# The delta rule's stages ranked 150 places later, background pieces re-spread, 32x32 bursts cut in halves

## The chip, the cores and the metric

The kernel runs on one core of one Trainium2 chip, as one program. The metric is the device time of an execution in microseconds; smaller is better. Times of several runs are given as a median, and traces are of one profiled execution.

## The reference

Two layers of a trunk over 256 tokens of width 2048, with 256 context tokens that only the first layer reads. Both layers take their shifts, scales and gates from a small vector times a large matrix (`w_ada`).

- Layer 0: a windowed attention with 8 heads beside a gated delta rule with 8 heads in two directions, an output projection, then a gated feed-forward block of width 5632.
- Layer 1: a Fourier mix over tokens and channel groups, a projection (`w_fourier`), then a second such feed-forward block.

```python
mx = jnp.split(silu_c @ w_ada[layer] + b_ada[layer], N_MOD, axis=-1)
h_x = modulate(rms_norm(x, g_pre_mix[layer]), mx[0], mx[1])
# layer 0: attention and delta rule, merged by w_out;  layer 1: fourier_mix(h_x) @ w_fourier
x = x + mx[2] * rms_norm(y_x, g_post_mix[layer])
f_x = swiglu(modulate(rms_norm(x, g_pre_ffn[layer]), mx[3], mx[4]), w_gate, w_up, w_down)
x = x + mx[5] * rms_norm(f_x, g_post_ffn[layer])
```

The delta rule works in chunks: each chunk needs a unit triangular solve, `sol = triangular_solve(I + m, rhs)`, and then a short scan over the chunks carries a state from one to the next.

## The kernel before

**Weights.** All large products are made in a split form: each weight tile (`raw`, 128x1024, 512 KB) is loaded on SyncE's queue (L188), copied to a rounded part `whi` on ScalarE (L198) and its remainder `wlo` (L204) on VectorE or GpSimd, and every product is three matmuls (L431 to L435, or L930 to L932). In the mixer of layer 0 `MSHARE` is 1, so GpSimd makes every `wlo` there. A load takes a buffer of the ring `raw` (4 buffers); while no pace is set, two in five take one of `araw` (2 buffers, L187).

**Background pieces.** What the layers need of `silu_c @ w_ada` beyond the first two vectors is cut into 320 pieces (L278 to L292): a load of 512 KB into `araw` on SyncE's queue (L286) and one product with a sum on VectorE (L275). Thirty-two pieces make one modulation vector. They are written into the program at a pace: `every(us)` (L148) says that a piece is written each time the kernel's own clock has gone on by so many microseconds. This clock (L131) is advanced by each matmul as it is written, by its columns over 2400, four times that for plain f32. The mixer's pace is `MRATE` (4.3, after a quiet start of 16), that of the output projection's first three strips `ORATE` (4.0), of layer 0's feed-forward block `F0RATE` (3.9), of the Fourier projection's first three strips `FRATE` (0, none), of layer 1's block `F1RATE` (10). `ada_until(n)` (L303) writes at once whatever is missing of the first n vectors: before the last strip of the output projection n is 3, of layer 0's down projection 6, of the Fourier projection 9 (L1183), and before that projection's first strip 7 (L1407).

**Delta rule.** Heads go in four groups g of two. Stage a (`gdn_a`, L636) makes a group's decay factors, its two sets of triangles and the inverse of their 16x16 blocks on VectorE (L737 to L744), with two trips through DRAM (L722 and L731, L750); stage b (`gdn_b`, L753) grows the inverses from 16 to 32, 64 and 128, and runs the scan over four chunks (L856 to L910). The step from 16 to 32 is made of 32x32 products in plain f32: 64 into `pQ` (L772 to L775), a copy of them to `Q5` (L777), then twice 64 into `pP` (L779 to L788). A stage issues its DMAs on ScalarE's queue, one of four stores of L750 on SyncE's, and its two fills with zeros on GpSimd (L726, L794).

**Order.** Stages, evacuations and attention are generators in a list `todo`; after each step of a projection `step()` (L592) resumes those whose time by the kernel's own clock has come, and what they write is placed there in the program. The number of microseconds that a generator yields, times `YS` = 1.2, is the wait until it is resumed. A planner then orders each engine's instructions: of those that are ready in its own model of the run, it takes the one with the lowest rank, and ranks are given in the order of writing. On VectorE the order is the written one between `in_order(True)` and `in_order(False)`, which holds from the first tile of a feed-forward block to the last strip of its down projection (L1262, L1184); the mixer and the Fourier stage are left to the planner.

Of the kernel before, what the change touches and what calls it, by code (L numbers as in the profile page):

```python
# [38 lines left out]
YF = 18  # L39
ORATE = 4.0  # L40
F0RATE = 3.9
FRATE = 0
F1RATE = 10.0
LD1 = 3
LD2 = 4
LD3 = 3
LD4 = 6
YSUB = 3
MAN = False
MAN2 = True  # L50
YEV = 1.3
# [3 lines left out]
PSPLIT = 0.25  # L55
NACT = 2
MSHARE = 1.0
MRATE = 4.3

WHO = 'pd' * 16  # L60
PRE = (4, 4, 4, 4)
# [11 lines left out]
def trunk(ctx: ExitStack, tc: tile.TileContext, a: dict, dbg=None, stop=None):  # L73
# [10 lines left out]
    def T(shape, tag, bufs, dt=F32):  # L84
        uid[0] += 1
        return sb.tile(list(shape), dt, tag=tag, bufs=bufs, name=f"{tag}_{uid[0]}")
# [28 lines left out]
    def e2(shape, dt=F32):  # L115
        return T(shape, "E2", 3, dt)
# [8 lines left out]
    def sm():  # L125
        uid[0] += 1
        return ps.tile([P, 512], F32, tag="sm", bufs=4, name=f"sm_{uid[0]}")
# [3 lines left out]
    def mm(out, l, r, start, stop):  # L131
        clock[0] += max(64, int(np.prod(r.shape[1:]))) * (4 if r.dtype == F32 else 1) / 2400.0
        nc.tensor.matmul(out, l, r, start=start, stop=stop)  # L133
# [14 lines left out]
    def every(us):  # L148

        pace[:] = [us, clock[0] + us]  # L150
# [3 lines left out]
    def in_order(on):  # L154

        if held:
            held.pop().__exit__(None, None, None)
        if on:
            held.append(tc.manual_schedule(engines={mybir.EngineType.DVE}))
            held[0].__enter__()  # L160
# [136 lines left out]
    def bg(n):  # L297
        for _ in range(n):
            if ada_n[0] < 320:
                next(ada_it)  # L300
                ada_n[0] += 1
# [287 lines left out]
    def add(gen, name=None):  # L589
        todo.append([gen, clock[0], name])  # L590

    def step():  # L592

        while pace[0] and pace[1] <= clock[0]:
            pace[1] += pace[0]
            bg(1)
        for t in list(todo):
            if t[1] <= clock[0]:
                d = next(t[0], None)
                if d is None:  # L600
                    todo.remove(t)
                    done.add(t[2])
                else:
                    t[1] = clock[0] + d * YS

    def drain(name=None):
        if name is not None and name in done:
            return
        while todo and (name is None or name not in done):
            clock[0] = max(clock[0], min(t[1] for t in todo))  # L610
            step()

    def gdn_proj(g):
        for fin, base, n in ((fin_k, 8, 2), (fin_v, 16, 2), (fin_q, 0, 1)):
            for hh in range(2):
                if (base + hh, g) == (8, 1):
                    continue
                p = acc()
                for hf in range(2):
                    w = load_w(a["w_gdn"][base + 2 * g + hh, hf])  # L620
                    for kk in range(8):
                        k = hf * 8 + kk
                        sl = slice(kk % 4 * P, (kk % 4 + 1) * P)
                        if n == 2:
                            mm3w(p, w[kk // 4], sl, k, k == 0, k == KC - 1)
                        else:
                            mm3(p, w[kk // 4], sl, 0, k, k == 0, k == KC - 1, 0)
                        step()
                add(fin(g, hh, p))
        add(gdn_a(g), f"a{g}")  # L630
        add(gdn_b(g), f"b{g}")

    def bl(i, n=32):
        return slice(n * i, n * i + n)

    def gdn_a(g):  # L636
# [100 lines left out]
        for k in range(15, 0, -1):  # L737
# [5 lines left out]
            if k % 4 == 0:  # L743
                yield YSUB  # L744
        V.tensor_copy(Y2[:, 1], Y.rearrange("p r c -> p c r"))
# [7 lines left out]
    def gdn_b(g):  # L753
# [18 lines left out]
        for d in range(2):  # L772
            for e in range(8):
                for b in range(4):
                    mm(pQv[bl(b), d, e], Zc[bl(b), d, e], YD[bl(b), 1, d, e], True, True)  # L775
        Q5 = e2([P, 2, 8, 32])
        V.tensor_copy(Q5, pQv)  # L777
        yield 2
        for i in (1, 0):  # L779
            pP = sm()  # L780
            pPv = pP.rearrange("p (d e f) -> p d e f", d=2, e=8)
            for d in range(2):
                for e in range(8):
                    for b in range(4):
                        x_, y_ = Q5[bl(b), d, e], YD[bl(b), 0, d, e]
                        if i == 1:
                            x_, y_ = y_, x_
                        mm(pPv[bl(b), d, e], x_, y_, True, True)  # L788
            (pP0, pP1) = (pPv, pP1) if i == 0 else (None, pPv)
        for i, p_ in ((0, pP0), (1, pP1)):  # L790
            V.tensor_tensor(out=YD[:, i], in0=YD[:, i], in1=p_, op=ALU.subtract)
# [121 lines left out]
    def proj(warr, npair, lhs, tiles, kept=None, nkeep=0, last=0):  # L913


        out = {t: acc() for t in tiles}
        second = kept is not None and tiles[0] > 0
        ks = range(npair)
        if second and last:
            ks = [npair - 1, *range(npair - 1)]  # L920
        for kp in ks:
            w = kept[kp] if second and kp in kept else load_w(warr[kp])
            if kept is not None and not second and (kp < nkeep or last and kp == npair - 1):
                kept[kp] = w
            for kk, (wh, wl) in enumerate(w):
                k = 2 * kp + kk
                first, final = kp == ks[0] and kk == 0, kp == ks[-1] and kk == 1
                for t in tiles:
                    h, l = lhs(k, t)
                    mm(out[t], h, wh, first, False)  # L930
                    mm(out[t], h, wl, False, False)
                    mm(out[t], l, wh, False, final)  # L932
                    step()
        return out
# [111 lines left out]
    add(fin_k(1, 0, p1))  # L1046
    add(gdn_a(0), "a0")
    add(gdn_b(0), "b0")
    every(MRATE)
    pace[1] += QUIET  # L1050
# [6 lines left out]
    seq.extend(a["w_att"][i, j] for i in range(1, 5) for j in range(8))  # L1057
    in_order(MAN)
    for g in range(1, 4):
# [296 lines left out]
    ab = {}  # L1356

    def over_d(g, t):

        if t == 0:  # L1360
            if g % 3 == 0:
                ab[0] = [zt([P, 3, 258], F32R) for _ in range(2)]
            dst = [ab[0][i][:, g % 3] for i in range(2)]
        else:
            r_ = T([P, 2, 258], "OG", 2, F32R)
            dst = [r_[:, i] for i in range(2)]
        ab[g, t] = dst
        p = sm()
        i = 0
        for kc in range(2):  # L1370
            src = hsl(2 * g + kc, t)
            for x_, y_ in three:
                mm(p[:, 0:258], src[x_], DD[y_][:, kc, :], i == 0, i == 5)
                i += 1
        split(*dst, p[:, 0:258])
# [19 lines left out]
    for g in range(9):  # L1395
# [6 lines left out]
        for h in range(FAHEAD, 8):  # L1402
            if g == h - 2:
                over_d(h, 0)
    every(FRATE)
    pool_share[0] = 0.0
# [123 lines left out]
```

## Time and profile before

| | us |
|---|---|
| median of 3 runs | 2509.49 |
| lowest and highest run | 2507.83, 2510.64 |
| the profiled execution | 2512.88 |
| its span in the trace | 2511.1 |
| TensorE matmul busy | 2386.3 (95%) |
| VectorE busy | 1778.5 (71%) |
| ScalarE busy | 1286.7 (51%) |
| GpSimd busy | 303.5 (12%) |

The profiled execution is 3.4 us (0.13%) above the median. In the trace the mixer lies from about 165 to 765 us, the output projection from 768 to 860, layer 0's feed-forward block up to about 1600, the Fourier transforms from 1605 to 1653, their projection to about 1735, and layer 1's block from there to the end. In rows, PE is TensorE, DVE VectorE, ACT ScalarE, POOL GpSimd and SP SyncE. "<-" behind an instruction names what ended the idle time before it; "issue" says that the profile shows nothing that it waited for. A matmul in plain f32 stands in the trace as two.

### The profile page before, as it was taken

What the parts mean: (1) busy time and instruction counts of PE and PEld (TensorE: products, weight loads), DVE (VectorE), ACT (ScalarE), POOL (GpSimd) and SP (SyncE); (2) the same over time, 40 slices, a digit from 0 to 9 for tenths busy, and PEclk for the clock granted to TensorE, in tenths of its full rate; (3) what the DMA queues carried; (4) which work ended last, traced back from release to release, by engine and by line L of the source; (5) the groups of instructions that cost most, each with busy time, mean ns of one, the idle gap of its engine ahead of it and who ended that gap; (6) DMA issues with size and microseconds to landing.
All of it is one profiled execution on the core that took longest, in us unless ns stands there. A gap on an engine that the chain in (4) does not pass through costs nothing.

```text
span 2511.1 us, 39666 instructions
## 1 busy us (share of the span) xinstructions
PE 2386.3 (95%) x14536; PEld 1990.4 (79%) x14536; DVE 1778.5 (71%) x3231; ACT 1286.7 (51%) x2317; POOL 303.5 (12%) x254
## 2 busy tenths in 40 slices
PE   7999789888899999999999999899999999999997
PEld 6888678877687788888888887687888888888886
DVE  5889788879457677777777788748666666555556
ACT  5347434453575644545455454746554544455455
POOL 1004334245430100000000000102000000000001
PEclk8999899999899999999999999999999999999999
DMA  8886768687547488888999998446677777666665
GB/s 302 289 285 218 235 197 288 208 263 256 180 134 233 158 303 308 314 310 312 315 313 315 311 317 311 166 128 232 193 235 236 235 241 241 193 186 187 190 201 193
DMA packets 218483, 611.04 MB, mean 243 GB/s; under 512 B 68904, under 2 KB 69912, under 8 KB 217520
## 3 DMA queue, kind: packets, MB, share of 16 engines
q1 hardware_dynamic: 168016, 581.59, 69.2%
q10 hardware_dynamic: 46528, 15.21, 2.6%
q0 software_dynamic: 3744, 11.71, 1.4%
q8 instruction: 114, 1.87, 0.3%
q14 instruction: 81, 0.66, 0.1%
HBM read 595.03 MB, written 13.40 MB: 242 GB/s over the span
## 4 chain that ended last, share of the span: by engine, by line
PE 75%; DVE 11%; DMA 6%; issue 4%; ACT 2%; POOL 1%; SPq 0%; ACTq 0%; DVEq 0%; POOLq 0%
PE acc L133 66%; PE sm L133 8%; DMA araw<-in_ada_d 4%; DVE araw L275 3%; DVE C L524 1%; POOL wlo L204 1%; DVE wlo L204 1%; PE sm L1248 1%; DVE S L1165 1%; DMA OG<-in_ada_s 1%; DMA T<-dz 1%; DVE K L719 0%; DVE T L740 0%; DVE T L742 0%; ACT whi L198 0%
## 5 line engine op out<-in xcount | busy, mean ns | idle before, releaser
L198 ACT ACTIVATE whi<-raw 128x512 fp32r<-128x512 f32 (+1 forms) x1306 | 819.0, 630 | 870.8 <-DVE wlo L204 470.3
L204 DVE TENSOR_TENSOR wlo<-raw,whi 128x512 fp32r<-128x512 f32 x1140 | 780.4, 692 | 443.9 <-ACT whi L198 442.1
L133 PE MATMUL acc<-whi,S 128*128 128x512 f32 x3312 | 1053.7, 396 | 2.6 <-ACT whi L198 2.6
L133 PEld LDWEIGHTS acc<-whi,S 128*128 128x128 f32 x3312 | 626.1, 189 | 135.9 <-ACT whi L198 3.0
L133 PE MATMUL acc<-wlo,S 128*128 128x512 f32 x1656 | 650.8, 393 | 3.8 <-DVE wlo L204 2.5
L275 DVE SCALAR_TENSOR_TENSOR araw<-araw,cb 128x1024 f32<-128x1024 f32 x320 | 414.4, 1296 | 58.2 <-DMA araw<-in_ada_d 57.7
L133 PEld LDWEIGHTS acc<-wlo,S 128*128 128x128 f32 x1656 | 313.1, 189 | 73.8 <-DVE wlo L204 2.9
L204 POOL TENSOR_TENSOR wlo<-raw,whi 128x512 fp32r<-128x512 f32 x166 | 242.6, 1474 | 554.7 <-ACT whi L198 546.1
L133 PE MATMUL acc<-S,whi 128*128 128x256 f32 x1152 | 223.8, 289 | 3.4 <-DVE K L489 3.0
L133 PEld LDWEIGHTS acc<-S,whi 128*128 128x128 f32 x1152 | 187.2, 196 | 3.9 <-issue 3.5
L133 PE MATMUL acc<-S,wlo 128*128 128x256 f32 x576 | 165.4, 287 | 3.0 <-POOL wlo L204 2.9
L1125 POOL DMA_DIRECT2D drow<-K x4 | 2.0, 508 | 1276.3 <-DVE K L1123 1276.3
L133 PE MATMUL acc<-whi,ZT 128*128 128x512 f32 x384 | 122.1, 391 | 0.0
L133 PEld LDWEIGHTS acc<-S,wlo 128*128 128x128 f32 x576 | 112.8, 196 | 4.2 <-POOL wlo L204 4.0
L133 PE MATMUL acc<-whi,KCH 128*128 128x512 f32 x320 | 109.4, 398 | 1.1 <-ACT whi L198 1.1
L133 PE MATMUL acc<-whi,A 128*128 128x512 f32 x312 | 106.0, 395 | 0.0
L133 PE MATMUL acc<-whi,T 128*128 128x512 f32 x296 | 99.5, 392 | 0.0
L133 PEld LDWEIGHTS acc<-whi,ZT 128*128 128x128 f32 x384 | 72.1, 188 | 15.3
L133 PE MATMUL acc<-wlo,KCH 128*128 128x512 f32 x192 | 77.2, 402 | 4.3 <-DVE wlo L204 4.1
L133 PE MATMUL acc<-wlo,ZT 128*128 128x512 f32 x192 | 75.5, 393 | 0.0
L133 PEld LDWEIGHTS acc<-whi,KCH 128*128 128x128 f32 x320 | 61.4, 192 | 14.9 <-ACT whi L198 1.5
L133 PE MATMUL acc<-wlo,T 128*128 128x512 f32 x176 | 68.9, 391 | 0.0
(441 smaller groups left out, 2810.2 us busy)
## 6 DMA issues: line engine op xcount, KB each, us to landing
raw<-in_w_gu SPq DMA_DIRECT2D x347, 512.0 KB, 4.4
araw<-in_ada_d SPq DMA_DIRECT2D x320, 512.0 KB, 4.8
raw<-in_w_dn SPq DMA_DIRECT2D x179, 512.0 KB, 4.4
raw<-in_w_att SPq DMA_DIRECT2D x40, 512.0 KB, 4.3
raw<-in_w_gdn SPq DMA_DIRECT2D x34, 512.0 KB, 4.6
raw<-in_w_out SPq DMA_DIRECT2D x30, 512.0 KB, 3.7
ZT<-in_ada_s SPq DMA_DIRECT2D x24, 512.0 KB, 4.6
raw<-in_w_four SPq DMA_DIRECT2D x21, 512.0 KB, 3.6
```

Of the source, the lines that this page charges most:

```text
L133: nc.tensor.matmul(out, l, r, start=start, stop=stop)
L198: S.activation(hi[:, :w], raw[:, c:c + w], AF.Copy)
L204: eng.tensor_sub(lo[:, :w], raw[:, c:c + w], hi[:, :w].bitcast(F32))
L275: V.scalar_tensor_tensor(out=junk, in0=w, scalar=1.0, in1=rows, op0=ALU.mult, op1=ALU.mult, accum_out=dst)
L524: V.scalar_tensor_tensor(out=ca[:, :, lo:hi], in0=pv[:, :, lo + o:hi + o], scalar=wconv[:, blk, j:j + 1], in1=ca[:, :, lo:hi], op0=ALU.mul ...
L1125: nc.gpsimd.dma_start(drow.rearrange("h k p -> (h k) p"), gt)
L1165: V.scalar_tensor_tensor(out=x[:, t, sl], in0=y[:, t, sl], scalar=r, in1=x[:, t, sl], op0=ALU.mult, op1=ALU.add)
L1248: nc.tensor.transpose(p[:, i * P:(i + 1) * P], hv[t][:, i * P:(i + 1) * P], ident)
```

## The change

- Each time a generator named a0 to a3 or b0 to b3 is resumed, what it writes gets a rank 150 places later (`LATER`), its DMAs and fills included.
- In stage b the 64 products of `pQ` and the two times 64 of `pP` are each cut into halves of 32 by direction `d`; between the halves, and between the two sets of `pP`, the generator yields 0.5.
- `MRATE` goes from 4.3 to 6.6 and `FRATE` from 0 to 5.0.

```diff
-FRATE = 0
+FRATE = 5.0
+LATER = 150
-MRATE = 4.3
+MRATE = 6.6
@@ step()
-                d = next(t[0], None)
+                if t[2] and t[2][0] in "ab" and len(t[2]) == 2:
+                    with tc.high_priority(-LATER):
+                        d = next(t[0], None)
+                else:
+                    d = next(t[0], None)
@@ gdn_b, pQ
             for e in range(8):
                 for b in range(4):
                     mm(pQv[bl(b), d, e], Zc[bl(b), d, e], YD[bl(b), 1, d, e], True, True)
+            if d == 0:
+                yield 0.5
@@ gdn_b, pP
                         mm(pPv[bl(b), d, e], x_, y_, True, True)
+                if d == 0 or i == 1:
+                    yield 0.5
```

## Rows read from the trace of the kernel before

**Rows 1.** the page's first line: the span

```profile
span 2511.1 us, 39666 instructions
```

**Rows 2.** stretches: busy us per engine (instructions), granted clock, DMA share, GB/s

```profile
185.00:765.00 580.00, 504.65 (x5432) 438.73 (x5430) 446.61 (x985) 299.69 (x607) 235.27 (x181) 0.93 0.70 222
425.00:436.00 11.00, 7.85 (x246) 7.55 (x235) 9.61 (x18) 3.34 (x8) 0.81 (x1) 0.69 0.84 273
540.00:662.00 122.00, 101.68 (x1011) 80.35 (x998) 95.47 (x195) 53.26 (x114) 66.40 (x52) 0.92 0.84 268
662.00:768.00 106.00, 99.51 (x1003) 78.97 (x1003) 59.79 (x187) 76.39 (x167) 28.82 (x27) 0.98 0.39 130
1565.00:1655.00 90.00, 79.01 (x491) 69.04 (x490) 60.52 (x120) 54.62 (x112) 12.80 (x10) 0.96 0.38 131
1655.00:1730.00 75.00, 75.00 (x327) 60.89 (x326) 46.35 (x72) 41.57 (x73) 6.40 (x6) 1.00 0.68 224
```

**Rows 3.** line 275 by stretch: count, duration ns min/median/max, first and last start

```profile
L275 DVE SCALAR_TENSOR_TENSOR araw<-araw,cb x96: 1205/1224/4106, 165.9 to 544.5; 128x1024 f32<-128x1024 f32 x96
L275 DVE SCALAR_TENSOR_TENSOR araw<-araw,cb x28: 1199/1222/2304, 544.5 to 658.5; 128x1024 f32<-128x1024 f32 x28
L275 DVE SCALAR_TENSOR_TENSOR araw<-araw,cb x161: 1206/1218/1227, 882.3 to 1564.2; 128x1024 f32<-128x1024 f32 x161
L275 DVE SCALAR_TENSOR_TENSOR araw<-araw,cb x2: 1218/1218/1219, 1712.2 to 1713.9; 128x1024 f32<-128x1024 f32 x2
L275 DVE SCALAR_TENSOR_TENSOR araw<-araw,cb x32: 1214/1218/1219, 1790.4 to 2128.4; 128x1024 f32<-128x1024 f32 x32
```

**Rows 4.** VectorE's waits, 165 to 662 us: total us, times, longest

```profile
DVE araw L275 <- DMA araw<-in_ada_d: 54.6, 44, 4.1
```

**Rows 5.** the chain that ended last, shares of 540 to 662 us

```profile
by line: issue 18.3%; DMA araw<-in_ada_d 14.3%; PE acc L133 12.4%; DVE araw L275 11.6%; PE sm L133 9.1%; POOL wlo L204 8.9%; DVE K L719 2.5%; DVE C L954 1.9%; DVE Zc L718 1.7%; PE sm L986 1.2%; ACT C L1027 1.2%; PE sm L1031 1.1%; DVE gsc L6
```

**Rows 6.** TensorE's waits, 185 to 765 us: total us, times, longest

```profile
PE sm L133 <- DVE rowhl L143: 12.5, 2, 10.6
PE sm L133 <- issue: 11.0, 4, 3.2
PE sm L133 <- DVE St L894: 7.9, 6, 3.5
```

**Rows 7.** VectorE in order of time, 300 to 309 us: start, us, what

```profile
300.97 2.22 DVE L275 SCALAR_TENSOR_TENSOR araw<-araw,cb 128x1024 f32<-128x1024 f32 x1 [1.58 <-DMA araw<-in_ada_d]
306.13 2.06 DVE L275 SCALAR_TENSOR_TENSOR araw<-araw,cb 128x1024 f32<-128x1024 f32 x1 [2.94 <-DMA araw<-in_ada_d]
308.23 0.68 DVE L143 TENSOR_TENSOR rowhl<-sm,rowhl 4x512 fp32r<-4x512 f32 x1
```

**Rows 8.** TensorE in order of time around two bursts: start, us, what

```profile
308.96 0.79 PE L133 MATMUL sm<-rowhl,selr 36*128 36x512 f32 x1 [10.59 <-DVE rowhl L143]
319.32 1.55 PE L133 MATMUL sm<-E,T 32*32 32x32 f32 x128
320.73 0.38 PE L133 MATMUL sm<-T,E 32*32 32x32 f32 x22
324.17 1.09 PE L133 MATMUL sm<-T,E 32*32 32x32 f32 x106 [3.06 <-issue]
329.21 0.40 PE L133 MATMUL acc<-S,whi 128*128 128x256 f32 x2
...
431.61 0.63 PE L133 MATMUL acc<-S,whi 128*128 128x256 f32 x2
```

**Rows 9.** a group of 32x32 products, 185 to 765 us: count, busy, mean, idle

```profile
L133 PE MATMUL sm<-T,E 32*32 32x32 f32 x512 | 6.9, 208 | 11.0 <-issue 11.0
```

**Rows 10.** DMA queue of kind instruction: packets, MB, share

```profile
q8 instruction: 114, 1.87, 0.3%
```

**Rows 11.** delta rule's last output (L908) and last gate (L994), 690 to 768 us

```profile
L908 DVE SCALAR_TENSOR_TENSOR OG<-sm,gsc,OG x8: 339/343/351, 734.2 to 749.9; 128x128 f32<-128x128 f32 x8
L994 ACT ACTIVATE C<-acc x4: 594/598/598, 702.4 to 750.8; 128x512 f32<-128x512 f32 x4
```

## The prediction, made before the changed kernel ran

> **What bounds the kernel now.** I read the page first, for the span [rows 1], then TensorE's waits by stretch, then the stretches themselves, and last the order of time around the longest waits. Through the two feed-forward blocks TensorE has next to no idle time; the change writes nothing else there. What is left is the mixer. From 185 to 765 us TensorE is busy 504.7 of 580 us, so 75 us are idle, and its granted clock is 0.93, so another 0.07 x 580 = 41 us of full clock are missing [rows 2]. The clock has two levels, 1.2 and 2.4 GHz, and it is low behind the waits: after one of them two matmuls of 256 columns take 0.63 us where they take 0.40 elsewhere [rows 8].
>
> Three things make these waits. First, the background pieces. VectorE takes its queue in order; in the mixer it stands still 54.6 us for pieces whose load has not landed [rows 4], and what is queued behind them waits too. The reader sees it at 300 us: two pieces, with waits of 1.58 and 2.94 us and 2.22 and 2.06 us of work, lie ahead of the split of `rowhl` at 308.23 [rows 7], for which TensorE has been idle 10.59 us [rows 8]. Second, the chain of the delta rule itself, as in the waits for `St` [rows 6]. Third, the bursts of 32x32 products: 11.0 us in four gaps of about 3 us that are put down to "issue" [rows 6, 9], each in the middle of a burst [rows 8].
>
> Where no piece runs, this is nearly gone. From 662 to 768 us the last stage b, the attention and the gates run together, and TensorE idles 6.5 of 106 us at a clock of 0.98; from 540 to 662, with pieces, it idles 20.3 of 122 us at 0.92 [rows 2].
>
> **Part 1, the pieces.** Of 320 pieces 161, 2 and 32 run after 860 us, so 125 run in the mixer [rows 3]. Fifteen belong to the output projection: three strips of 16 x 2 x 3 matmuls of 512 columns are 61.4 us of the kernel's own clock, over 4.0. The mixer wrote 110, so its clock is 16 + 110 x 4.3 = 489 us or a little more; at 6.6 it writes (489 - 16)/6.6 = 72. With 15 that makes 87; the rule of three vectors before the last strip adds 9, to 96. Layer 0's block adds its 161 as before, to 257. The Fourier projection then writes 61.4/5.0 = 12 in its three strips, 269, and 19 more before the last, 288; layer 1 has its 32. So **29 pieces leave the mixer and 29 more run around the Fourier projection**, 31 in place of 2.
>
> They will not thin out evenly. In the mixer the planner pulls pieces ahead as soon as a buffer of `araw` is free: all 125 are done by 660 us, though the last are written with the projection that runs after 768 [rows 3]. So I expect 96 at the same spacing, done near 540, where the 96th stands now [rows 3], and a stretch of 540 to 662 without any. There the chain holds loads of pieces for 14.3% and their products for 11.6% of 122 us, 31.6 us or 1.09 us a piece [rows 5]: the upper bound. The nearer row is the next stretch: its idle share would leave 7.5 of 20.3 us, of which one burst's gap of about 2.6 is not the pieces' doing, so 10 us, and the clock from 0.92 to 0.98 another 7. The split of the weights on GpSimd (8.9% of the chain [rows 5]) is late next, so I take **-10 us**, bounds -32 and 0.
>
> Where they arrive: the planner is free from layer 0's last strip to layer 1's block, so they will be pulled ahead to 1565 and run through the tail, the transforms and the projection. SyncE's queue has room: the DMA share is 0.38 there and 0.68 in the projection. VectorE is busy 60.5 of 90 us, then 46.4 of 75 [rows 2], and 31 x 1.3 = 40 us fit into the 58 that are left. In the projection TensorE is busy 75.0 of 75 us [rows 2] and covers them; if that cover is gone, each costs what one costs in the mixer. In the tail and norm, where TensorE idles 11 us of 90, some twenty pieces stand in the queue of the engine that the chain runs on; a quarter of them on the chain at 1.3 us is 6. The last burst of 19 is written before the modulation that needs it, and with 2 buffers it would hold up layer 1's norm only if it were not pulled ahead. While a pace is set the Fourier weights no longer use `araw`, so 4 buffers instead of 6; layer 0's block runs TensorE without idle time on 4. I take **+5**, bounds 0 and 31 x 1.09 = +34.
>
> **Part 2, the halves.** One `pQ` or `pP` set of 64 products is 128 matmul records in 1.55 us [rows 8], with as many weight loads 256 instructions. The queue of kind "instruction" moved 114 packets of 16.4 KB [rows 10] for 2 x 14,536 TensorE instructions, 255 a packet; so three sets empty three such packets within a few microseconds, and the gap comes in the third. I read the gap as the wait for the next one. Of the Trainium skill, "Runtime: NRT & Kernel Launch", section "Instruction fetch mechanics", says that the sequencer fetches the next 16 KiB page while it executes the current one and that crossing a page is mostly hidden. By that rule the halves would gain nothing (a rival below); the row speaks against it, since the gap stands inside a set whose operands are there.
>
> Each group gets four cuts: one in `pQ`, three in `pP`. A yield of 0.5 is 0.6 us of the clock, so one step of a projection (0.64 us) comes between. Three in the `pP` sets put 1.9 us of useful work where 3 us were idle: four groups, 7.7 us. The clock behind a burst (0.69 over 11 us, 3.4 us lost [rows 2]) may come back in part, some 3 us of 4 x 3.4. I take **-10**, bounds -25 (11.0 + 13.6) and +8, the same 7.7 us laid on stage b if its chain were what ends last.
>
> **Part 3, the ranks.** From 185 to 765 us some 5,300 instructions were written (acc matmuls once, plain f32 halved, of 7,205 records [rows 2]), 9 a microsecond; an estimate of 150 ranks is thus 16 us. Projections, evacuations and weight splits written up to 16 us later now go first when they are ready. On TensorE that puts work in front of products whose operands arrive late (12.5 us for `rowhl`, 7.9 for `St` [rows 6]). What moves with them: on VectorE the stages' work behind `conv` and splits; on ScalarE's queue the loads and the DRAM trips of both stages behind copies of `whi`; on SyncE's one store behind weight and piece loads; on GpSimd two fills behind `wlo`. They do not fall behind the pieces, which are written more than 16 us after the time at which they run. All 75 us of idle time less the 11 of the bursts are the upper bound; the lower is the whole lag of 16 us at the mixer's end. Between them I take a quarter of the 20.4 us for `rowhl` and `St`: **-5**, bounds -64 and +16.
>
> **Sum.** -10 + 5 - 10 - 5 = -20 us: the profiled 2512.9 becomes 2492.9, of which 1.8 lie outside the span [rows 1]. That execution is 3.4 us over the median; from the median, 2509.5 - 20 = **2489.5 us**.
>
> **Rivals.** *The lag ends last* (slower). The last output of the delta rule comes at 749.9 us and the last gate at 750.8 [rows 11], with the merge right behind: both ends meet. If projections run ahead and are used up, stage b of the last group stands alone at the end with its 16 us. Then the pieces and half the stall time (-8) no longer shorten what ends last: +16 + 5 - 8 = +13, 2522 us. It decides once idle time after 662 us grows beyond its 6.5 us by more than what the stretches before save. Against it: TensorE's order goes by ranks, and the last b had slack enough to be shared out among attention. *The pieces cost the same elsewhere*: -32 + 34 instead of -5 for the two ends of their move gives 2509.5 + 2 - 10 - 5 = 2496 us; for it speaks that the chain at 1565 to 1655 goes through VectorE. *Fetch is hidden anyway*: without the -10 of the halves 2499 us. *The change does little of what it says*: nothing else was ready in the planner's model, halves run back to back, and the pieces' -10 and +5 shrink to nothing: 2509 us.
>
> **How the numbers follow.** The forecast has 0.56 (2470 to 2503), the lag 0.16 (2514 to 2530), the same cost elsewhere 0.12 (2490 to 2502), hidden fetch 0.10 (2495 to 2504), little done 0.06 (2505 to 2514). What this kernel's measurement can tell from no change is about 0.2%, 5 us. Faster: 0.54 + 0.12 + 0.09 = 0.75 with rounding, slower 0.16 + 0.01 = 0.17, within 0.08. The range from 2463 to 2519 leaves out a part of the lag's case and the best of the forecast, some 0.17.
>
> **What would show it.** The pieces: none of L275 between about 545 and 860 us, 31 between 1565 and 1735, and an idle share of 540 to 660 us like that of 662 to 768. The halves: sets of 64 records in the order of time, and less than 11 us under "issue". The ranks: the waits for `rowhl` and `St` shorter, the last output of the delta rule no later than the last gate. I am wrong if the idle time after the last projection grows, or if the tail before 1605 us lengthens by more than 6 us.

## The result, and the profile after

The changed kernel takes 2648.1 us (median of 4 runs, 2646.5 to 2649.9) against 2509.9 us before (4 runs): a ratio of 1.056, 95% interval 1.054 to 1.057. It is 138 us slower, where 20 us faster was forecast, and far above the range.

Nine tenths of it lie ahead of the end of the output projection, the rest in the Fourier stage. I use one mark per stage: the start of the first residual update on VectorE after each projection. The mark behind the output projection moves from 835.8 to 955.9 us, by 120.1. From there to the same mark of layer 0's block it is 752.1 us in both traces, from there to the Fourier projection's mark 159.7 us after 146.3, and the rest is 776.9 us in both: 120.1 + 13.4 = 133.5 us, the difference of the two spans.

First the page of the kernel after: span, TensorE's busy tenths and its granted clock in 40 slices of 66 us.

```profile
span 2644.6 us, 39659 instructions
PE   8999889999989899999999999989999999999998
PEclk8999988579599999999999999999999999999999
```

TensorE seems busier than before (95% of its span then, 96% now), so its busy share shows nothing of the loss. The clock line does: the slices from 397 to 727 us read 8, 5, 7, 9, 5. The same in stretches of the mixer (busy us of PE, PEld, DVE, ACT, POOL with their instructions, granted clock, DMA share, GB/s):

```profile
185.00:765.00 580.00, 536.30 (x4325) 427.88 (x4324) 342.77 (x740) 217.50 (x430) 203.95 (x157) 0.81 0.54 172
...
400.00:500.00 100.00, 98.67 (x848) 79.96 (x847) 51.41 (x107) 32.65 (x62) 28.97 (x22) 0.74 0.57 189
500.00:600.00 100.00, 96.44 (x647) 76.29 (x647) 49.95 (x106) 29.49 (x69) 21.53 (x17) 0.75 0.40 129
600.00:700.00 100.00, 95.93 (x751) 60.88 (x751) 38.45 (x84) 32.34 (x59) 42.24 (x31) 0.75 0.45 144
```

Against [rows 2] TensorE is busy longer in the same 580 us (536.3 after 504.7) and gets through fewer instructions (4325 after 5432); VectorE, ScalarE and GpSimd all did less too. Up to the mark it runs the same 5915 matmuls, first before, then after:

```profile
165.00:835.80 670.80, 594.70 (x5915) 515.35 (x5913) 505.94 (x1094) 349.20 (x699) 244.06 (x189) 0.94 0.70 223
165.00:955.90 790.90, 734.00 (x5915) 583.40 (x5914) 464.92 (x1035) 341.49 (x690) 235.93 (x189) 0.86 0.53 170
```

They take 139.3 us more busy time, while the idle time falls from 76.1 to 56.9 us: what the mixer and the output projection lose lies wholly inside TensorE's busy time. From 400 to 700 us the granted clock is 0.74 to 0.75 with 1 to 4 us idle in each 100. What fills TensorE's time there is seen only in the order of time (start, us, what):

```profile
444.17 0.28 PE L134 MATMUL acc<-S,wlo 128*128 128x256 f32 x1
444.29 0.40 PE L134 MATMUL acc<-S,whi 128*128 128x256 f32 x2
444.52 0.28 PE L134 MATMUL acc<-S,wlo 128*128 128x256 f32 x1
...
446.23 0.24 PE L134 MATMUL sm<-T,Zc 32*32 32x32 f32 x2
446.40 0.38 PE L134 MATMUL acc<-S,whi 128*128 128x256 f32 x1
446.71 0.24 PE L134 MATMUL sm<-T,Zc 32*32 32x32 f32 x2
...
447.20 0.24 PE L134 MATMUL sm<-T,Zc 32*32 32x32 f32 x2
447.38 0.38 PE L134 MATMUL acc<-S,wlo 128*128 128x256 f32 x1
...
448.35 0.58 PE L134 MATMUL acc<-S,whi 128*128 128x256 f32 x1
448.86 0.31 PE L134 MATMUL sm<-T,Zc 32*32 32x32 f32 x2
449.10 0.58 PE L134 MATMUL acc<-S,wlo 128*128 128x256 f32 x1
```

Until 444.6 us the projection's products follow each other every 0.12 us. From 445.9 each is followed by one product of 32x32 (two records, as it is plain f32): a pair comes every 0.49 us, and from 448.35, where the clock has fallen to its lower level of 1.2 GHz, every 0.75 us. Before, the 64 products of such a set ran in one piece, 1.55 us for 128 records [rows 8].

The pieces and the waits went largely as they were meant to. The pieces (L276 now), count and first and last start:

```profile
L276 DVE SCALAR_TENSOR_TENSOR araw<-araw,cb x96: 1207/1225/2343, 148.3 to 634.5; 128x1024 f32<-128x1024 f32 x96
L276 DVE SCALAR_TENSOR_TENSOR araw<-araw,cb x161: 1204/1218/1225, 1002.4 to 1684.2; 128x1024 f32<-128x1024 f32 x161
L276 DVE SCALAR_TENSOR_TENSOR araw<-araw,cb x31: 1211/1224/1229, 1727.0 to 1826.8; 128x1024 f32<-128x1024 f32 x31
```

The 96th starts at 634.5 us, since the whole mixer is stretched; without the ranks (no_later, below) it starts at 531.5, as forecast. Then the waits of TensorE on which the forecast rested, 185 to 880 us (us in all, times, longest):

```profile
PE sm L134 <- DVE rowhl L144: 7.9, 1, 7.9
...
PE sm L134 <- DVE St L903: 4.5, 4, 2.6
...
PE sm L134 <- issue: 1.3, 1, 1.3
```

All three are shorter than in [rows 6]: 7.9 after 12.5, 4.5 after 7.9, 1.3 after 11.0. Last, the counterpart of [rows 11], the delta rule's last output and the last gate:

```profile
L917 DVE SCALAR_TENSOR_TENSOR OG<-sm,gsc,OG x16: 334/343/352, 753.9 to 873.5; 128x128 f32<-128x128 f32 x16
L1003 ACT ACTIVATE C<-acc x4: 589/598/599, 800.3 to 854.1; 128x512 f32<-128x512 f32 x4
```

The two no longer meet: the delta rule ends 19.4 us behind the last gate.

### The profile page after: what moved, and what is told of

It reads as the page before. It is cut to its first block, busy times and chain, and to the rows that moved or that the text cites. A ratio compares the mean times of both kernels' runs of the same rounds, so it can differ in the third digit from the quotient of the medians.

```text
span 2644.6 us, 39659 instructions
## 1 busy us (share of the span) xinstructions
PE 2531.0 (96%) x14536; PEld 2060.9 (78%) x14536; DVE 1768.9 (67%) x3231; ACT 1279.7 (48%) x2308; POOL 296.3 (11%) x254
## 4 chain that ended last, share of the span: by engine, by line
PE 74%; DVE 6%; DMA 4%; ACT 1%; issue 1%; ACTq 0%; POOL 0%; DVEq 0%
PE acc L134 66%; PE sm L134 6%; DMA araw<-in_ada_d 2%; DVE araw L276 1%; PE sm L1257 1%; DVE S L1174 1%; DVE wlo L205 1%; DVE C L525 1%; DVE T L745 0%; DMA araw<-in_w_dn 0%; DVE T L747 0%; DMA T<-dz 0%; PE sm L1040 0%; DMA A<-dq 0%; ACT whi L199 0%
## 5 line engine op out<-in xcount | busy, mean ns | idle before, releaser
L199 ACT ACTIVATE whi<-raw 128x512 fp32r<-128x512 f32 (+1 forms) x1324 | 831.7, 630 | 1011.1 <-PE acc L134 498.0
L205 DVE TENSOR_TENSOR wlo<-raw,whi 128x512 fp32r<-128x512 f32 (+1 forms) x1158 | 795.1, 694 | 451.9 <-ACT whi L199 449.6
L134 PE MATMUL acc<-whi,S 128*128 128x512 f32 x3312 | 1074.3, 401 | 8.0 <-DVE T L745 3.8
L134 PE MATMUL acc<-wlo,S 128*128 128x512 f32 x1656 | 660.7, 399 | 3.0 <-POOL wlo L205 3.0
L276 DVE SCALAR_TENSOR_TENSOR araw<-araw,cb 128x1024 f32<-128x1024 f32 x320 | 402.6, 1259 | 60.8 <-DMA araw<-in_ada_d 60.3
L205 POOL TENSOR_TENSOR wlo<-raw,whi 128x512 fp32r<-128x512 f32 x166 | 235.7, 1430 | 623.2 <-ACT whi L199 610.2
L134 PE MATMUL acc<-S,whi 128*128 128x256 f32 x1152 | 263.1, 316 | 2.6 <-DVE K L490 2.6
L134 PEld LDWEIGHTS acc<-S,whi 128*128 128x128 f32 x1152 | 200.8, 206 | 8.9 <-issue 3.1
L134 PE MATMUL acc<-S,wlo 128*128 128x256 f32 x576 | 182.3, 317 | 1.1 <-POOL wlo L205 0.9
L134 PEld LDWEIGHTS acc<-S,wlo 128*128 128x128 f32 x576 | 118.9, 206 | 4.8 <-POOL wlo L205 1.7
```

Of the source, the lines that this page charges most:

```text
L199: S.activation(hi[:, :w], raw[:, c:c + w], AF.Copy)
L205: eng.tensor_sub(lo[:, :w], raw[:, c:c + w], hi[:, :w].bitcast(F32))
L276: V.scalar_tensor_tensor(out=junk, in0=w, scalar=1.0, in1=rows, op0=ALU.mult, op1=ALU.mult, accum_out=dst)
```

## The experiments

**How the sets come apart.** The rank counter, printed while the program is written, is raised by 150 on entering `high_priority(-LATER)` and is set back on leaving. So a resumed generator's instructions do not go behind all that is written later; they get the same ranks as what the projection writes about 150 ranks later. Where 64 products of a stage and a projection's products hold the same ranks and both are ready, the planner's order has one of each in turn, as in the rows above.

**The theories.** *Shape:* what costs time is the alternation of 32x32 and 64x64 products with full ones, on TensorE itself and through the clock. *Lag:* the stages come later and the last one stands alone at the end, with TensorE idle beside it. *Halves or pieces:* one of the other two parts does it. The table shows the runs; "mark" is that behind the output projection; "changes" counts, in TensorE's order of time from 165 us to the mark, how often a product of 32x32 or 64x64 follows a full one or the reverse; "at 1.2 GHz" adds up the granted clock's records there. Mark and the two columns behind it are those of the profiled execution.

| kernel | median us | ratio, 95% | mark us | changes | us at 1.2 GHz |
|---|---|---|---|---|---|
| before | 2509.2 | | 835.8 | 52 | 78.5 |
| after | 2648.1 | 1.056 (1.054 to 1.057) | 955.9 | 530 | 228.7 |
| later_only | 2679.2 | 1.068 (1.065 to 1.071) | 1002.2 | 622 | 269.7 |
| no_later | 2507.7 | 1.000 (0.998 to 1.001) | 818.5 | 80 | 64.9 |
| bursts_first | 2583.5 | 1.030 (1.027 to 1.033) | 895.4 | 278 | 174.1 |
| bursts_later | 2541.9 | 1.013 (1.009 to 1.017) | 864.3 | 150 | 92.2 |
| small_first | 2529.0 | 1.008 (1.006 to 1.011) | 837.1 | 58 | 85.3 |
| halves_only | 2513.3 | 1.002 (1.001 to 1.003) | 835.7 | 82 | 75.1 |
| rates_only | 2506.6 | 0.999 (0.998 to 1.000) | 817.5 | 52 | 61.4 |
| f0_takes | 2500.7 | 0.998 (0.997 to 0.999) | 819.1 | 80 | 58.0 |
| f0_whole | 2502.6 | 0.998 (0.996 to 0.999) | 820.5 | 52 | 68.3 |
| f0_earlier | 2566.7 | 1.020 (1.016 to 1.024) | 886.8 | 184 | 136.5 |

(The kernel before is 2508.4 to 2509.9 us in the groups of runs that these belong to; each ratio is against its own group.)

### The ranks alone, and all but the ranks

later_only is the kernel before with `LATER` alone; no_later is the changed kernel without it:

```diff
-                if t[2] and t[2][0] in "ab" and len(t[2]) == 2:
-                    with tc.high_priority(-LATER):
-                        d = next(t[0], None)
-                else:
-                    d = next(t[0], None)
+                d = next(t[0], None)
```

> The kernel before with the later rank of stages a and b alone (150 places), no halves, old rates. Theory, mixing: in a stretch that runs at the later rank the counter is set back afterwards, so the stage's products share their ranks with projection matmuls that are written next, and the planner lays the 32x32 products one by one between them; that is slow and holds the clock low. It expects nearly the whole loss here: 2600 to 2650 us. Rival, lag: the chain of the delta rule comes later and stands alone at the mixer's end; it expects the same time here, but with TensorE idle at the end. Rival, pieces: the loss comes from the new rates; it expects 2500 to 2520.

> The changed kernel with the later rank taken back: halves and new rates alone. Mixing and lag both expect the loss of the mixer to be gone: 2495 to 2530 us, with some 13 us more in the Fourier stage than before and the mixer within 15 us of before. Pieces expects 2600 or more.

The ranks alone cost 6.8%, more than the whole change and more than the range given for it; without them it is even with before. TensorE's idle time up to the mark is 71.8 us in later_only, 76.1 in before, so the loss is no wait at the end, as *lag* has it. The loss is the ranks', and halves and rates give back 2679.2 - 2648.1 = 31 us of it. Where the halves yield, another generator or a projection step may be written in between, so fewer ranks of a set are shared; that was not taken apart.

### Which instructions of the stages

The ranks move some thousand instructions of all engines. bursts_first keeps them, but puts the three sets of the step from 16 to 32 ahead of everything; bursts_later ranks only these sets later, in the kernel before. The first of the sets in bursts_first (the other two likewise):

```diff
+            with tc.high_priority(LATER + 400):
                 for e in range(8):
                     for b in range(4):
                         mm(pQv[bl(b), d, e], Zc[bl(b), d, e], YD[bl(b), 1, d, e], True, True)
```

> The changed kernel, with the loops of 32x32 products of the 16-to-32 step alone given a rank far ahead, so that each half runs together as soon as its operands are there; all else of stages a and b keeps the later rank. Mixing expects most of the loss to be gone: 2500 to 2550 us, the clock from 400 to 700 us back above 0.9. Lag expects it to stay: 2610 to 2650.

> The kernel before with the later rank given to the loops of 32x32 products of the 16-to-32 step alone, everything else of stages a and b at its old rank, no halves, old rates. Mixing expects most of the loss: 2580 to 2650 us. Lag expects little, since only three short sets of products a group move: 2505 to 2530.

Both move in the direction of the shape theory and neither reaches its end: bursts_first gives back 64.6 of the 140 us between after and no_later, bursts_later loses 32.7 us by itself. Both medians lie between the ranges of the two theories. The clock of bursts_first from 400 to 700 us is still 0.75 to 0.82. The trace of bursts_first says why it stops there (TensorE in order of time): the alternation goes on with the next step's set, the products with `ZT`.

```profile
459.16 0.58 PE L134 MATMUL acc<-S,whi 128*128 128x256 f32 x1
459.67 0.31 PE L134 MATMUL sm<-T,ZT 32*32 32x32 f32 x2
459.91 0.58 PE L134 MATMUL acc<-S,whi 128*128 128x256 f32 x1
```

So small_first puts all sets of 32x32 and 64x64 products of stage b ahead, in the same way, and leaves everything else of the stages 150 ranks later.

> The changed kernel with all sets of 32x32 and 64x64 products of stage b given a rank far ahead, so that each set runs together; all else of stages a and b keeps the later rank. By the order that the planner writes, TensorE goes 58 times between a small shape and a full one, against 530 in the changed kernel, 278 with the first three sets alone kept together, 80 without the later rank. Mixing, at about 0.3 us a switch in the runs so far, expects the mixer within 15 us of the one without the later rank: 2495 to 2530 us. Lag (the rest of the chain still comes later) expects that what was left with the first three sets kept together stays: 2560 to 2590.

The changes of shape fall from 530 to 58, the time at 1.2 GHz from 229 to 85 us, and the mark comes back from 955.9 to 837.1. Its stretches show the same stage at nearly the full clock:

```profile
400.00:500.00 100.00, 90.99 (x1270) 86.70 (x1270) 76.92 (x163) 50.32 (x101) 36.84 (x28) 0.95 0.77 260
500.00:600.00 100.00, 87.94 (x1036) 74.14 (x1034) 54.36 (x132) 47.46 (x95) 53.55 (x42) 0.91 0.63 195
```

TensorE is idle more than after (9.0 us of the first 100 instead of 1.3) and gets through 1270 products instead of 848. Of the 137.4 us between the marks of no_later and after, 118.8 go with the order of the small sets, and 18.6 remain with them in one piece. (The execution of small_first is 6.5 us below its median. By the medians some 25 us remain: 21.3 between the two, and a Fourier stage 3.8 us shorter.)

These 18.6 us are not a lag that could be read off at the end. 6.0 of them are busy time, with 20.4 us more at 1.2 GHz, and 12.6 are idle time. The idle time is under "issue" (16.5 us after 4.1, 185 to 770 us), first small_first, then no_later:

```profile
PE sm L134 <- issue: 9.3, 5, 3.1
...
PE acc L134 <- issue: 7.2, 3, 4.1
```

```profile
PE sm L134 <- issue: 4.1, 4, 2.0
```

Six of the eight gaps of small_first stand inside a small set or within 2 us behind one. The delta rule's last output does come later: at 754.5 us with the last gate at 738.3, in no_later at 724.8 and 720.5. But in the last 128 us ahead of the mark TensorE idles 7.7 us after 4.8. So what shows of the lag there is 3 us; no run has the lag alone.

Per change of shape TensorE's busy time grows by 135.0 / 472 = 0.29 us from small_first to after, 25.3 / 98 = 0.26 from before to bursts_later, 170.7 / 570 = 0.30 from before to later_only. That the time goes with the count is shown. The clock is a part of it, at most half of the 150.2 us that after spends more at 1.2 GHz than before, 75 of the 139.3 us; this is an estimate, as if all that ran there had taken half the time at the upper level. The next run asks whether the change of shape is the price, or only goes along with it.

### The change of shape by itself

switch_cost is a program of its own with none of the reference's work, executed once: full products (256 columns, in the split form's type) alone, then one to one with plain f32 32x32 products on the four diagonal blocks, then the same two kinds in groups of 64, then one to one with plain f32 products of the full shape and 32 columns.

```python
for i in range(2 * N): big(big0)
for i in range(N): big(big1); small(s1, i)
for i in range(0, N, 64):
    for j in range(64): big(big2)
    for j in range(64): small(s2, j)
for i in range(N): big(big3); full(s3, i)
```

> A kernel that computes nothing of the reference, only sets of matmuls on one engine: 384 products with 256 columns alone; 192 of them, each followed by one 32x32 product; the same in groups of 64 and 64; 192, each followed by a 128x128 product with 32 columns; 192 alone. Mixing expects the second set to take at least 0.25 us more a pair than the third, at the same clock, and the clock to fall in it; the fourth tells whether it is the shape (as cheap as the third) or the small size (as dear as the second).

The granted clock of its 300 us in 40 slices, then TensorE in order of time, one to one with 32x32, in groups, and one to one with the full shape:

```profile
PE   1999999999999999999999999999999999999993
PEclk9999999965555555555555558999999999999998
```

```profile
59.41 0.38 PE L42 MATMUL big_by<-r,w 128*128 128x256 f32 x1
59.72 0.24 PE L47 MATMUL sm_by<-xs 32*32 32x32 f32 x2
59.90 0.38 PE L42 MATMUL big_by<-r,w 128*128 128x256 f32 x1
...
62.35 0.58 PE L42 MATMUL big_by<-r,w 128*128 128x256 f32 x1
62.86 0.31 PE L47 MATMUL sm_by<-xs 32*32 32x32 f32 x2
63.10 0.58 PE L42 MATMUL big_by<-r,w 128*128 128x256 f32 x1
...
188.06 7.93 PE L42 MATMUL big_groups<-r,w 128*128 128x256 f32 x64
195.93 1.29 PE L47 MATMUL sm_groups<-xs 32*32 32x32 f32 x128
197.14 7.93 PE L42 MATMUL big_groups<-r,w 128*128 128x256 f32 x64
...
209.64 0.36 PE L42 MATMUL big_by<-r,w 128*128 128x256 f32 x1
209.84 0.30 PE L51 MATMUL sm_by<-xs 128*128 128x32 f32 x2
209.98 0.36 PE L42 MATMUL big_by<-r,w 128*128 128x256 f32 x1
```

The pitch is the kernel's own: 0.49 us a pair, then 0.75 us. Alone, 384 full products take from 7.2 to 54.9 us, 0.124 each; the 192 pairs in groups take from 176.9 to 206.1, 0.152 a pair (three groups each, part of the first still at the lower clock; the 64 pairs from 188.06 to 197.14 take 0.142 each). So alternating adds 0.49 - 0.15 = 0.34 us a pair, 0.17 a change, at 2.4 GHz, and 0.60 a pair, **0.30 a change**, where the clock is at 1.2 GHz (against groups at the upper level, so the slower clock is counted in). The instructions are the same in both, so their order is the price.

With small products of the full shape a pair takes 0.34 us, between the two cases that were expected, and the weight loads are busy 65.96 of 66.00 us (below); the clock stays at its upper level. So plain f32 and 32 columns in turn with the split form explain neither the 0.49 us nor the clock. At least 0.15 us a pair, and the fall of the clock, go with the two shapes; whether the rest does too can't be told here, since a smaller cost would be hidden behind the weight loads. The two stretches side by side:

```profile
62.30:181.00 118.70, 118.70 (x477) 74.81 (x476) 0.76 (x2) 0.00 (x0) 0.00 (x0) 0.50 0.00 1
206.00:272.00 66.00, 66.00 (x614) 65.96 (x601) 0.84 (x3) 0.00 (x0) 0.00 (x0) 1.00 0.01 1
```

TensorE counts as busy for every microsecond of the first, and the clock is at its lower level; it was at the upper one before, when the same full products ran alone, and is again once those of the next set run alone.

Of the Trainium skill, "TensorEngine Tiling (Array Packing)", section "Tiling Modes" (key properties), says that changing the tiling mode, unlike changing the tile, drains TensorE. It gives no price. These runs agree in that going back and forth costs time, 0.17 us a change at 2.4 GHz by the rows above; that the price is a drain, no row shows.

### The halves and the rates, each alone

halves_only is the kernel before with the four yields, rates_only with `MRATE` 6.6 and `FRATE` 5.0.

> The kernel before with the halves alone. The prediction's part 2 expects 10 us less in the mixer (bounds 25 less, 8 more) and shorter gaps under issue; that fetching instructions is hidden anyway expects no change: within 5 us of before.

> The kernel before with the new rates alone (6.6 in the mixer, 5.0 in the Fourier projection), no halves, no later rank. If the 17 us that the mixer gained with halves and rates are the pieces', as the halves alone suggest, the mixer is 12 to 22 us shorter than before here too, the Fourier stage about 13 longer, and the whole 2500 to 2512 us. If they came from halves and rates together, the mixer is as before and the whole 2515 to 2525.

**Halves.** TensorE's wait under "issue" falls from 11.0 us [rows 6] to this:

```profile
PE sm L133 <- issue: 5.2, 3, 3.1
```

It is as short in no_later (4.1) and f0_takes (4.3), which have the halves too, and 11.8 and 12.6 us in rates_only and f0_whole, which have whole sets. Yet the mark is 0.1 us earlier and the kernel 0.1 to 0.3% slower. There are 30 changes of shape more (82 after 52); at 0.17 us each they are 5.1 us, as much as the 5.8 us of waits that went. The numbers fit the two marks; that one paid for the other is not shown. The execution of before is 3.4 us above its median and this one 2.4 below, so by the medians the halves cost about 5 us, and these were not found.

**Rates.** The mark comes 18.3 us earlier, and the Fourier stage is 10.7 us longer (157.0 after 146.3). The execution of before is 3.4 us above its median and this one 3.1 below; by the medians, 2.7 us apart, the mixer gains about 13. The stretch between the mark of layer 0's block and the Fourier projection, and that projection up to its mark, first in before (from 1588), then in rates_only (from 1569):

```profile
1588.00:1655.00 67.00, 56.78 (x400) 52.54 (x399) 41.73 (x89) 36.57 (x80) 4.62 (x4) 0.95 0.22 72
1655.00:1734.00 79.00, 79.00 (x344) 64.15 (x343) 49.95 (x78) 43.61 (x78) 7.69 (x7) 1.00 0.70 229
```

```profile
1569.00:1640.00 71.00, 56.67 (x395) 52.39 (x394) 61.56 (x125) 36.60 (x80) 3.94 (x3) 0.93 0.58 197
1640.00:1726.00 86.00, 81.78 (x351) 65.10 (x350) 61.77 (x102) 44.48 (x80) 8.33 (x8) 1.00 0.81 282
```

TensorE does the same 57 us of work in 71 us instead of 67, VectorE 61.6 us instead of 41.7; in the projection behind it TensorE is busy 81.8 of 86 us, where before had 79 of 79. VectorE waits 18.4 us in the two stretches for pieces that have not landed, in a stage in which before has two pieces [rows 3].

### Giving the pieces to layer 0's block instead

Layer 0's block keeps TensorE busy all the time (1100 to 1500 us in after: 400.00 of 400.00). f0_takes is no_later with

```diff
-F0RATE = 3.9
-FRATE = 5.0
+F0RATE = 3.3
+FRATE = 0
```

and f0_whole the same without the halves (the kernel before with `MRATE` 6.6 and `F0RATE` 3.3).

> Halves and the slower pace in the mixer without the later rank, and no pieces in the Fourier projection (pace 0 as before): layer 0's feed-forward block takes the 29 pieces at a pace of 3.3 in place of 3.9. If the 13 us that the Fourier stage lost are the pieces', they come back, and the block's TensorE, busy all the time, covers the pieces: 2485 to 2500 us. Rival: the block's loads then come late (its DMA share is 0.88 already) and it gets longer by the same or more: 2505 to 2530.

> The kernel before with a pace of 6.6 in the mixer and 3.3 in layer 0's feed-forward block, the sets of 32x32 products whole and nothing in the Fourier projection. If the halves are worth nothing, it is as fast as the version with halves: 2496 to 2506 us. If they help once fewer pieces run beside them, it is 5 to 10 us slower than that.

The mixer keeps its gain (marks 819.1 and 820.5), the Fourier stage is back at 145.9 and 146.3 us, and layer 0's block pays 4.4 us for its 190 pieces instead of 161 (756.5 and 756.4 after 752.1). Both are 0.25% faster than before (0.1 to 0.4%), the best of the series: 2500.7 and 2502.6 us, the first just above the range given for it. Halves or whole sets makes no difference that these runs can tell.

f0_earlier asks for the reverse, ranks 150 places earlier for the stages, on f0_whole:

```diff
+LATER = -150
```

> The same with stages a and b ranked 150 places earlier instead of later. The counter is set back here too, so ranks are shared with matmuls written before that still wait: by the planner's order TensorE goes 184 times between a small shape and a full one, against 52. Mixing, at 0.3 us a switch, expects 132 x 0.3 = 40 us more than with the ranks untouched: 2525 to 2550. Lag expects no loss, since the chain now comes sooner: 2485 to 2505.

It loses 2.0% (1.6 to 2.4; four runs from 2545.8 to 2569.7 us), more than either theory gave. Ranks are shared in this direction too: 184 changes of shape after 52, and 136.5 us at 1.2 GHz after 68.3. At 0.30 us the 132 changes are 40 of the 66 us by which the mark moves; TensorE has also more idle time from 165 us to the mark (85.4 us after 68.9), and waits that were shorter before are ahead in its list, 185 to 820 us:

```profile
PE sm L991 <- DVE C L959: 10.3, 3, 5.8
PE sm L134 <- DMA T<-dy: 8.2, 1, 8.2
```

(In f0_whole 6.4 and 4.4 us.) With 16.5 us of idle time that leaves 10 us, which were not followed up: the busy time grows by 49.8 us, 0.38 a change.

## Why the prediction was wrong

**What bounds the kernel.** The waits named were there, and they did fall: TensorE's idle time from 165 us to the mark is 56.9 us after, 76.1 before. The step that failed stands at the start: "75 us are idle ... another 41 us of full clock are missing" took idle time and the clock behind it as all there was to win or lose, and the time in which TensorE is busy as a constant. Busy time itself grew, from 594.7 to 734.0 us for the same 5915 matmuls. The sign to look for was how products of two shapes lie to each other, and [rows 8] show that before had them in whole sets.

**Part 1, pieces: right in place, larger in size.** The counts came as worked out, 96, 161, 31 and 32. "-10 us" for the mixer measured -18.3 between two executions (rates_only; no_later has -17.3) and about -13 to -15 by the medians, inside -32 to 0: some 0.4 to 0.6 of the upper bound, where a third was taken. "+5" for the Fourier stage measured +10.7, or +13.8 with the halves (160.1 us), inside 0 to +34. The term that was too small is "a quarter of them on the chain": the work and waits of the pieces ran on into the projection, where the forecast had them covered by TensorE, and TensorE stood still 4 of 86 us. The median moved by 2.7 us, not 5.

**Part 2, halves: wrong in worth.** "-10" measured -0.1 in the mixer between two executions and +0.17% (0.06 to 0.29), about +5 us, in all, within the bounds -25 to +8. The cuts did shorten the gaps under "issue", but that they are waits for packets of instructions, as the forecast had it, no run shows. The step that failed is "useful work where 3 us were idle": the work put between belongs to another shape, and each cut brings two changes. The time is thus that of the rival "fetch is hidden anyway", though its reason stays open: the gaps were there and were shortened by cuts, and what they wait for was not found.

**Part 3, ranks: wrong in mechanism.** The sentence "projections, evacuations and weight splits written up to 16 us later now go first when they are ready" treats a stage as a block that moves behind others. It does not go behind; it is mixed in with them, product by product. The bound "-64 and +16" therefore covered the lag only. Missing was the mixing: from small_first to after 472 changes and 118.8 us at the mark, in which the busy time grows by 135.0 us, 0.29 a change, and the idle time falls by 16.2. What the lag costs stays open; 18.6 us are left with the sets in one piece, most of them not a wait at the end. The forecast's 16 us for 150 ranks are also too few, since the stages' own instructions no longer advance the counter; by how much was not measured. The mixing could have been bounded beforehand: the Trainium skill's sentence on mode changes ("TensorEngine Tiling (Array Packing)", as above) speaks against this change and was not weighed, and three sets of 64 products in each of four groups, if all alternated, are 1536 changes, so even a tenth of a microsecond each would have been far above every other term.

**The rivals.** *The lag ends last* had the right sign, and its sign in the trace came true: the delta rule's last output 19.4 us behind the last gate, after 0.9 us ahead of it. But it gave +13 us by idle time, and TensorE's idle time fell. That it named the right sign is luck: what costs the time is another mechanism.

**In sum**, pieces and halves together leave no_later's 2507.7, even with before (rates_only alone -0.1%, halves_only +0.2%). The ranks add 137 us, the difference of the two marks: 2645, where 2648 was measured.

## What to carry to other kernels

Changing the rank of a group of instructions changes which of its neighbours they are mixed with, not only when they run: where ranks are shared, sets that were written in one piece come apart. On TensorE, look at the order of time for products of different shapes taken in turn, and keep each set of small ones together; busy share and waits don't show the loss; the granted clock, the number of products in a stretch and the busy time of a fixed number of products do. Background work is best given to a stage whose bound engine it does not touch, and its price there is to be measured (here 4.4 us for 29 pieces in layer 0's block, against 10.7 in the Fourier stage).

## What the chip showed that was not expected

- A product of 32x32 and a full one in turn take 0.49 us a pair at 2.4 GHz, where the same two in groups of 64 take 0.15. With the small one written in the full shape the pair takes 0.34 us, so in that program the padded form is the faster one in turn; the kernel was not run with it.
- The clock fell to 1.2 GHz while such an alternation ran and stayed there for 119 us, with TensorE busy 118.7 of 118.7 us. A busy share of 100% in the profile did not mean a full clock.
